# The end of a diffusion layer: last modulation as a row ahead of the turning, residual added in PSUM or by wide additions

## The chip, the cores and the metric

The kernel runs on one core of a Trainium2 chip. The metric is the device time of one execution in microseconds (us), lower is better. The engines of the core are named PE (matrix products; PEld is its weight load), DVE, ACT, POOL and SP (which mostly issues DMAs). PE writes to PSUM, a memory of eight banks of 128 partitions x 512 fp32 values; the other data lies in SBUF (128 partitions) or in HBM.

## The reference

One layer of a hybrid backbone, on 128 context tokens and 256 latent tokens, D_MODEL = 2048, all fp32. What matters here is the end:

```python
mod = jax.nn.silu(cond) @ lw['w_ada'] + lw['b_ada']
sh1, sc1, ga1, sh2, sc2, ga2 = [m[:, None, :] for m in jnp.split(mod, N_MOD, axis=-1)]
...
x = x + ga1 * rmsnorm(m, lw['norm_post_mix'])
h = rmsnorm(x, lw['norm_pre_ffn']) * (1.0 + sc2) + sh2
ff = (jax.nn.silu(h @ lw['w_ffn_gate']) * (h @ lw['w_ffn_up'])) @ lw['w_ffn_down']
x = x + ga2 * rmsnorm(ff, lw['norm_post_ffn'])
```

`cond` is one vector for all context tokens and another for all latent tokens, so the last factor, `ga2` times the gain of the norm, is one row of 2048 values for each of the two kinds. RMSNorm divides each token's row by the root of its mean square.

## The kernel before

**Tiling.** The 384 tokens are three blocks `t` of 128: block 0 is the context, blocks 1 and 2 are latent. The 2048 columns are 16 groups of 128 (index `k`) or 4 pieces of 512 (index `n` or `q`). Most of the kernel, and the residual `x1b` too, keeps columns on partitions and tokens along the free dimension; the output `yT` has that layout as well. The down projection of the FFN, in contrast, has tokens on partitions: `unit(t, n)` is the SBUF tile of 128 tokens x 512 columns in which the result of block `t`, piece `n`, is summed. So the end of the kernel has to *turn* each unit by PE, in four squares of 128x128.

**Weights.** They arrive by DMA as `raw` tiles of 512 KB in two buffers (L1654) or in resident slots `u...` (L1662). ACT rounds a tile to its high half `whi` (L1684), DVE subtracts to get the low half `wlo` (L1695), four buffers of each; PE multiplies high by high, high by low and low by high (L339). The FFN runs in 11 chunks of 512 hidden columns; steps "A" to "H" are the gate and up products, "D" the down product. In the order of pieces (0, 2, 1, 3) the last chunk's down product adds into the units; `add_last` (L1852, L1853) does this for a piece and has ACT sum the squares.

**The last modulation.** `ada_last` computes it in four quarters and leaves it in `mods[:, 5, k, c]`: partition = column within group `k`, `c` = 0 for context and 1 for latent. Its last write is DVE's at L1744. The resident slots 6 and 7 share the buffer `adacc` of an earlier phase.

**The end.** From `rest = d_order[2:]` on, the order on all engines and on SP is the order in which the code stands, as written by hand. Ahead of that line this holds for the other engines, while SP's DMAs are put in order by a scheduler, from when it expects their buffers and data to be ready. The last two pieces (1 and 3) are multiplied block by block (`last_products`), and the end of one block lies beside the products of the next:

- `norm(t)`: `most` and `factor` (root, ACT) and `inverse` (DVE) give the factor `r3[:, t]` of each token; `scale` multiplies the four pieces of the block by it, two on DVE (L1967), two on ACT (L1965).
- `turn(t, q)`: PE transposes the four squares of a piece (L1979) into one PSUM bank `py`. For block 2, pieces 0 and 2 are not scaled first: their squares are multiplied by `dg`, the identity times the factors, which turns and scales in one (L1981).
- `finals(t, q)`: for each of the four squares one DVE instruction, `x1b = py * mods + x1b` (`final`, L1992, 128x128). In some pieces ACT multiplies and POOL adds. For piece 3 of block 2 ACT multiplies four squares into `wide` (L2048) and DVE adds once (L2054).
- `store`: one DMA of 256 KB from SP for each piece (L1996), one from ACT.

PSUM banks come from two pools, `psm` with three and `pss` with five.

## Time and profile before

| what | value |
|---|---|
| median of 3 runs | 1921.23 us (1920.87 to 1922.34) |
| profiled execution, device time | 1922.69 us |
| its span in the trace | 1920.9 us |
| clock granted to PE | 1.0 |
| HBM read, written | 361.94 MB, 16.78 MB |
| mean DMA rate | 203 GB/s |

The profile is of one execution. "Span" is the time from its first to its last event in the trace; the device time has a little around it. Busy shares are means over the whole span, and the tail with which the change deals is under 1% of it, so it has to be read from the timeline and from windows of a few us. A row of the timeline gives start, duration, engine, line, operation, tiles, shape and, where instructions were merged, a count; in brackets stands how long the engine had been idle and what ended that. The chain of work is followed back from the last instruction, at each step to what released it.

### The profile page before, as it was taken

To read this page: it belongs to the slowest core of one execution; us is meant where nothing else is said; L and a number is where in the kernel's file an instruction comes from. 1 tells how busy PE (TensorE), PEld (TensorE's weight loads), DVE (VectorE), ACT (ScalarE), POOL (GpSimd) and SP (SyncE) were. 2 spreads that over 40 slices of the span, in tenths; PEclk is the share of its full clock that TensorE was granted. 3 is DMA by queue.
4 is the path that set the end of the run, shared out by engine and by line. 5 is a ranking of instruction groups with operands and counts; after the bars stand their busy time and mean duration, and the time that the engine had idled before them with its cause. 6 is when DMAs were issued, how large, how long until landed. Compare 5 with 4: busy or idle time off the path is not lost.

```text
span 1920.9 us, 27361 instructions
## 1 busy us (share of the span) xinstructions
PE 1901.7 (99%) x10318; PEld 1676.6 (87%) x10318; DVE 1650.9 (86%) x2168; ACT 999.4 (52%) x1428; POOL 82.7 (4%) x146
## 2 busy tenths in 40 slices
PE   8999999999999999999999999999999999999998
PEld 5679999999999999999988888888888788888886
DVE  5659897889868898987789989998998999887876
ACT  4235455545455654456456474556455545564544
POOL 0001111100000000104000000000000000000000
PEclk9999999999999999999999999999999999999999
DMA  9976766766657886656255656464746474736344
GB/s 390 400 280 226 261 224 227 269 211 207 215 180 236 285 297 227 211 201 224 68 178 160 189 148 199 142 191 143 224 127 210 122 229 114 221 92 198 92 153 145
DMA packets 237865, 389.70 MB, mean 203 GB/s; under 512 B 51189, under 2 KB 163925, under 8 KB 233381
## 3 DMA queue, kind: packets, MB, share of 16 engines
q1 hardware_dynamic: 218500, 330.02, 51.9%
q0 software_dynamic: 13952, 50.39, 8.5%
q10 hardware_dynamic: 5280, 7.55, 1.1%
q8 instruction: 81, 1.33, 0.3%
q14 instruction: 52, 0.42, 0.1%
HBM read 361.94 MB, written 16.78 MB: 197 GB/s over the span
## 4 chain that ended last, share of the span: by engine, by line
PE 84%; DVE 8%; DMA 4%; ACT 2%; issue 2%; SPq 0%; DVEq 0%; ACTq 0%
PE pmm L327 31%; PE pgu L339 24%; PE pdn L339 16%; PE pv L507 3%; DVE wlo L1695 2%; PE pgm L490 1%; DMA slab<-in_w_ada 1%; PE pf L1260 1%; PE pfo L1060 1%; PE pmm L1537 1%; DMA raw<-in_w_d 1%; DMA raw<-in_w_g 1%; ACT whi L1684 1%; DVE acc L1724 1%; DVE wlo L288 1%
## 5 line engine op out<-in xcount | busy, mean ns | idle before, releaser
L327 PE MATMUL pmm<-A_hi,whi 128*128 128x384 f32 x1088 | 366.9, 337 | 0.0
L327 PE MATMUL pmm<-A_hi,wlo 128*128 128x384 f32 x1088 | 364.2, 335 | 0.8 <-DVE wlo L288 0.8
L327 PE MATMUL pmm<-A_lo,whi 128*128 128x384 f32 x1088 | 364.1, 335 | 0.3 <-DVE A_lo L380 0.3
L1684 ACT CAST whi<-u 128x1024 fp32r<-128x1024 f32 x200 | 209.7, 1052 | 200.1 <-DVE u L1694 60.9
L1684 ACT CAST whi<-raw 128x1024 fp32r<-128x1024 f32 x175 | 183.8, 1050 | 189.8 <-DMA raw<-in_w_g 66.0
L1695 DVE TENSOR_TENSOR wlo<-u,whi 128x1024 fp32r<-128x1024 f32 x200 | 243.8, 1219 | 27.1 <-ACT whi L1684 21.3
L339 PE MATMUL pgu<-whi,A_lo 128*128 128x512 f32 x640 | 249.0, 389 | 0.0
L339 PE MATMUL pgu<-whi,A_hi 128*128 128x512 f32 x640 | 249.0, 389 | 0.0
L1695 DVE TENSOR_TENSOR wlo<-raw,whi 128x1024 fp32r<-128x1024 f32 x175 | 213.1, 1218 | 28.2 <-ACT whi L1684 18.7
L288 DVE TENSOR_TENSOR wlo<-raw,whi 128x1024 fp32r<-128x1024 f32 x165 | 200.6, 1219 | 31.0 <-ACT whi L301 30.7
L301 ACT CAST whi<-raw 128x1024 fp32r<-128x1024 f32 x151 | 157.9, 1049 | 123.2 <-PE pmm L327 42.9
L724 DVE SCALAR_TENSOR_TENSOR adacc<-adaw,spad,adacc 128x1024 f32<-128x1024 f32 x170 | 210.3, 1277 | 1.9 <-DMA adaw<-in_w_ada 1.7
L327 PEld LDWEIGHTS pmm<-A_hi,whi 128*128 128x128 f32 x1088 | 204.2, 188 | 3.3 <-issue 1.7
L327 PEld LDWEIGHTS pmm<-A_hi,wlo 128*128 128x128 f32 x1088 | 204.2, 188 | 1.4 <-DVE wlo L288 1.3
L327 PEld LDWEIGHTS pmm<-A_lo,whi 128*128 128x128 f32 x1088 | 204.4, 188 | 1.0 <-DVE A_lo L380 0.8
L339 PE MATMUL pdn<-whi,hid_hi 128*128 128x512 f32 x480 | 187.1, 390 | 0.6 <-DVE psums L1859 0.6
L339 PE MATMUL pgu<-wlo,A_hi 128*128 128x512 f32 x640 | 184.6, 390 | 2.2 <-DVE wlo L1695 2.2
L339 PE MATMUL pdn<-whi,hid_lo 128*128 128x512 f32 x480 | 186.8, 389 | 0.0
L339 PEld LDWEIGHTS pgu<-wlo,A_hi 128*128 128x128 f32 x640 | 119.7, 188 | 28.8 <-DVE wlo L1695 4.2
L339 PEld LDWEIGHTS pgu<-whi,A_hi 128*128 128x128 f32 x640 | 120.1, 188 | 25.0
L339 PEld LDWEIGHTS pgu<-whi,A_lo 128*128 128x128 f32 x640 | 120.1, 188 | 24.9
L339 PE MATMUL pgu<-whi,S 128*128 128x512 f32 x480 | 128.3, 389 | 0.0
(404 smaller groups left out, 3061.2 us busy)
## 6 DMA issues: line engine op xcount, KB each, us to landing
adaw<-in_w_ada POOLq DMA_DIRECT2D x96, 512.0 KB, 4.1
raw<-in_w_d SPq DMA_DIRECT2D x88, 512.0 KB, 3.9
slab<-in_w_ada SPq DMA_DIRECT2D x32, 1024.0 KB, 10.0
raw<-in_w_gate SPq DMA_DIRECT2D x64, 512.0 KB, 4.5
raw<-in_w_g SPq DMA_DIRECT2D x48, 512.0 KB, 3.7
raw<-in_w_u SPq DMA_DIRECT2D x48, 512.0 KB, 3.9
raw<-in_w_in SPq DMA_DIRECT2D x46, 512.0 KB, 4.3
u<-in_w_u SPq DMA_DIRECT2D x40, 512.0 KB, 4.7
```

The lines of the kernel that those rows point to most:

```text
L288: eng.tensor_sub(lo, raw, hi.bitcast(F32))
L301: ACT.copy(hi, raw)
L327: PE.matmul(dst, w[wi][:, k * n + n0 : k * n + n0 + P], x[xi][:, k0 + k, :], start=first and k == 0 and j == 0, stop=last and k == kts - 1 ...
L339: PE.matmul(dst, stat[x_][m], mov(w[w_], m), start=first and w_ == m == x_ == 0, stop=last and w_ == m == 1,)
L490: PE.matmul(pgv[q : q + 32, :], spad[:, k, :], slab[k // (KT // 2)][:, k % (KT // 2), :], start=k < 4, stop=k >= KT - 4,)
L507: PE.matmul(pv[2 * t + g], hT[x_][:, kb, t * P : (t + 1) * P], w_[:, g * 512 : (g + 1) * 512], start=kb == 0 and j == 0, stop=kb == KT - 1 ...
L724: DVE.scalar_tensor_tensor(acc[:, c, :], w, spad[:, k, c : c + 1], acc[:, c, :], op0=ALU.mult, op1=ALU.add,)
L1060: PE.matmul(p, w_of[0][:, i, k, g, :], x[:, :, lo:hi], start=kt == 0, stop=False)
L1260: PE.matmul(pf[:, 0 : 2 * HT], w[0][:, c], x[k], start=k == 0, stop=False)
L1537: PE.matmul(hp[u], hw[u][j][:, ((k - 1) % 8) * P : ((k - 1) % 8 + 1) * P], h2[m][:, k - 1, :], start=k == 1 and j == m == 0, stop=k == KT ...
L1684: ACT.copy(hi, src)
L1695: DVE.tensor_sub(lo, src, hi.bitcast(F32))
```

## The change

The latent row of the last modulation is written to HBM as a row (`m_d`, 2048 values, from `mods` with its columns on partitions) once `ada_last` is done, and is read back onto all 128 partitions as `mrow` (128x2048, in the buffer `adacc`) where `x1b` is loaded. In blocks 1 and 2, whose tokens all have this row, units can now be multiplied by it ahead of turning, as tokens x columns: `times_m`, or one fused instruction with the factor for block 1, piece 3. Pieces 0 and 1 of block 1 are turned and finished as before, with `mods`; so is all of block 0.

For four pieces (block 1: 2, 3; block 2: 1, 3) PE first puts the residual into the bank by a product of the identity with 512 columns of `x1b` (`old`), and the turning products add to it; ACT copies the bank to `x1b`. For pieces 0 and 2 of block 2 DVE adds the whole bank to `x1b` in one instruction. All of block 2 is turned by `dg`, so its units are not scaled.

```diff
+                mrow = adap.tile([P, D], F32, tag="adacc", name="mrow")
+                SP.dma_start(mrow, m_d.to_broadcast([P, D]))
                 ACT.activation(tmp1, eps_t, AF.Sqrt)
...
                 for _ in ada:
                     pass
+                m_d = dram.tile([1, D], F32, name="m_d")
+                SP.dma_start(m_d.rearrange("o (k p) -> (o p) k", p=P), mods[:, 5, :, 1])
...
-        def turn(t, q, diag=None):
-
+        def bank_of(t, q):
             pool = py_pools[t][q]
             py[t, q] = pool.tile([P, 4, P], F32, tag="side" if pool is pss else "mm", name="py")
+
+        def old(t, q):
+
+            bank_of(t, q)
+            PE.matmul(py[t, q], ident, y_of(t, q), start=True, stop=False)
+
+        def turn(t, q, diag=None):
+
+            added = (t, q) in py
+            if not added:
+                bank_of(t, q)
             for j in range(4):
                 src = unit(t, q)[:, j * P : (j + 1) * P]
                 if diag is None:
                     PE.transpose(py[t, q][:, j, :], src, ident)
                 else:
-                    PE.matmul(py[t, q][:, j, :], src, diag, start=True, stop=True)
+                    PE.matmul(py[t, q][:, j, :], src, diag, start=not added, stop=not added or j == 3)
+
+        def y_of(t, q):
+            return x1b[:, 4 * q : 4 * q + 4, t * P : (t + 1) * P]
+
+        def times_m(t, n):
+            DVE.tensor_mul(unit(t, n), unit(t, n), mrow[:, 512 * n : 512 * n + 512])
...
-            for n in range(4):
-                scale(ACT if n > 1 else DVE, t, n)
...
+        for t, n in ((2, 0), (1, 2), (2, 2)):
+            times_m(t, n)
         last_products(0, 0)
...
         norm(0)
+        for n in range(4):
+            scale(ACT if n > 1 else DVE, 0, n)
...
         norm(1)
+        scale(DVE, 1, 0)
+        scale(ACT, 1, 1)
+        scale(ACT, 1, 2)
+        f = unit(1, 3)
+        DVE.scalar_tensor_tensor(f, f, col(r3, 1), mrow[:, 3 * 512 :], op0=ALU.mult, op1=ALU.mult)
...
         add_last(2, rest[1], bk[2, 1], 3)
-        for q in range(2, 4):
-            turn(1, q)
+        times_m(2, 1)
+        for q in (2, 3):
+            old(1, q)
+            turn(1, q, ident)
+        for q in (1, 3):
+            old(2, q)
         factor(2)
-        finals(1, 2)
-        store(8, 12, 1, 2)
         inverse(2)
         DVE.tensor_scalar_mul(dg, ident, col(r3, 2))
-        scale(ACT, 2, 3)
-        scale(ACT, 2, 1)
-        finals(1, 3)
-        for q in (0, 3, 1, 2):
-            turn(2, q, dg if q in (0, 2) else None)
-        store(12, 16, 1, 2)
-        wide = ep[4].rearrange("p (j x) -> p j x", j=4)
-        for k in range(12, 16):
-            ACT.mul(wide[:, k - 12, :], py[2, 3][:, k - 12, :], mods[:, 5, k, 1:2])
-        finals(2, 0)
-        store(0, 4, 2, 3)
-        finals(2, 1)
-        store(4, 8, 2, 3)
-        last = x1b[:, 12:16, 2 * P : 3 * P]
-        DVE.tensor_add(last, last, wide)
-        store(12, 16, 2, 3, ACT)
-        finals(2, 2)
-        store(8, 12, 2, 3)
+        times_m(2, 3)
+        for q in range(4):
+            turn(2, q, dg)
+        for q in (2, 3):
+            ACT.copy(y_of(1, q), py[1, q])
+            store(4 * q, 4 * q + 4, 1, 2)
+        for q in range(4):
+            if q % 2:
+                ACT.copy(y_of(2, q), py[2, q])
+            else:
+                DVE.tensor_add(y_of(2, q), y_of(2, q), py[2, q])
+            store(4 * q, 4 * q + 4, 2, 3, ACT if q == 3 else SP)
```

How this moves instructions, at three places. First PE, behind the last two products with the weights (`pdn`, L339) at the end of the program; `py` are the banks, `ep_7646` is `dg`, `psums` are the units; lines 1979 and 1981 of before, 1983 (`old`) and 1995 (`turn`) of the change:

```order
-L1979 MATMUL py<-ident,psums 128x128 x8
-L1981 MATMUL py<-ep_7646,psums 128x128 x4
-L1979 MATMUL py<-ident,psums 128x128 x8
-L1981 MATMUL py<-ep_7646,psums 128x128 x4
-L2125 UNCONDITIONAL_BRANCH
+L1983 MATMUL py<-x1b,ident 128x512
+L1995 MATMUL py<-ident,psums 128x128 x4
+L1983 MATMUL py<-x1b,ident 128x512
+L1995 MATMUL py<-ident,psums 128x128 x4
+L1983 MATMUL py<-x1b,ident 128x512 x2
+L1995 MATMUL py<-ep_7646,psums 128x128 x16
```

Sixteen transposes and eight products by `dg` became four products of 512 columns, eight products by the identity and sixteen by `dg`, and all four wide ones stand ahead of the first product by `dg`.

Second SP's queue, from the last loads of up-weights on to the last loads of down-weights (`raw<-in_w_d`); first before, then the change:

```order
L1654 DMA raw<-in_w_u 128x4x256 x2
L1654 DMA raw<-in_w_d 128x2x512 x4
L1871 DMA x1b<-x_d 128x1536
L1654 DMA raw<-in_w_d 128x2x512
L1871 DMA x1b<-x_d 128x1536
L1654 DMA raw<-in_w_d 128x2x512
L1871 DMA x1b<-x_d 128x1536 x2
L1654 DMA raw<-in_w_d 128x2x512 x4
```

```order
L1654 DMA raw<-in_w_u 128x4x256 x2
L1654 DMA raw<-in_w_d 128x2x512
L1873 DMA mrow<-m_d 128x2048
L1654 DMA raw<-in_w_d 128x2x512 x2
L1871 DMA x1b<-x_d 128x1536
L1654 DMA raw<-in_w_d 128x2x512 x2
L1871 DMA x1b<-x_d 128x1536 x2
L1654 DMA raw<-in_w_d 128x2x512
L1871 DMA x1b<-x_d 128x1536
L1654 DMA raw<-in_w_d 128x2x512 x4
```

The load of `mrow` came between the first and the second of these down-weight loads, and the first and third pieces of `x1b` stand one weight load earlier.

Third SP's queue where the modulation has been completed, amid the products of the FFN:

```order
 L1654 DMA raw<-in_w_d 128x2x512
 L1662 DMA u_9282<-in_w_u 128x4x256
+L1925 DMA m_d<-mods 128x16x1
 L1654 DMA raw<-in_w_u 128x4x256
 L1662 DMA u_9280<-in_w_g 128x4x256
```

The store of `m_d` stands ahead of a load of up-weights, and nothing else moved there.

## The prediction

> **What bounds the kernel now.** I read the page's busy shares first, then the chain of work that ended last, then the timeline of the last 15 us.
>
> ```profile
> span 1920.9 us, 27361 instructions
> PE 1901.7 (99%) x10318; PEld 1676.6 (87%) x10318; DVE 1650.9 (86%) x2168; ACT 999.4 (52%) x1428; POOL 82.7 (4%) x146
> ```
>
> PE has work nearly everywhere, so before the end only what makes PE wait can move the time. The change works in the tail, after the last big products. There the chain of work leaves PE:
>
> ```profile
> 1874.65 26.63 PE pdn L339 x116
> ...
> 1909.70 0.60 DVE psums L1852
> ...
> 1910.38 0.73 ACT ep L1853 x2
> ...
> 1911.14 0.30 ACT r L1957
> ...
> 1911.66 0.30 DVE ep L2039
> ...
> 1912.09 1.15 PE py L1981 x8
> ...
> 1913.53 1.63 DVE x1b L1992 x6
> ...
> 1915.42 0.60 DVE x1b L2054
> 1916.02 1.04 DVE x1b L1992 x4
> ```
>
> Columns are start, duration, what. The last block's sum of squares is closed (1910.38), its root taken (1911.14), `dg`, the identity times the row factors, is ready at 1911.96, PE turns the blocks, and DVE finishes with the 128x128 `final` operations of L1992 until 1917.06. The last store is issued there (its row is below) and the span ends 3.84 us later. I take these 3.84 us as they are. So today the tail from 1912 is **DVE-bound**: DVE runs nearly without a gap, while PE is done at 1915.
>
> ```profile
> 1912.00:1915.00 3.00, 2.90 (x24) 2.73 (x24) 2.72 (x11) 2.14 (x6) 0.00 (x0) 1.00 0.81 235
> 1915.00:1918.00 3.00, 0.00 (x0) 0.00 (x0) 2.06 (x7) 0.00 (x0) 0.00 (x0) 1.00 0.83 237
> L1996 SPq DMA_DIRECT2D out_yT<-x1b x11: 372/373/492, 1905.3 to 1917.1; - x11
> ```
>
> (The windows give PE, PEld, DVE, ACT, POOL busy, then the clock: 1.00, no throttling. The third row gives the first and last start of a store.)
>
> **The change, part by part.** On DVE 20 `final` operations of the second and third token blocks go; two wide additions come in place of one, with five multiplications by `mrow` and one fused scale. ACT loses two scalings of 128x512 and four 128x128 multiplications, and gains four copies of 128x512. PE gets the residual of four 128x512 pieces (`old`), and 24 small matmuls by a diagonal, where it had 16 transposes and 8 such matmuls. So the question is what PE's list behind its last product costs.
>
> ```profile
> 1908.78 0.62 PE L339 MATMUL pdn<-wlo,hidE 128*128 128x512 f32 x2
> 1909.24 1.03 PE L1979 MATMUL py<-ident,psums 128*128 128x128 f32 x8
> 1913.93 1.06 PE L1981 MATMUL py<-ep,psums 128*128 128x128 f32 x8
> L1981 PE MATMUL py<-ep,psums x16: 275/275/348, 1912.1 to 1914.7; 128*128 128x128 f32 x16
> 8.72 4.68 PE L408 MATMUL px<-spad,ones 128*128 128x384 f32 x14
> L408 PE MATMUL px<-spad,ones x22: 486/486/980, 4.2 to 12.9; 128*128 128x384 f32 x22
> ```
>
> *Small matmuls.* The 8 matmuls of L1981 left 16 records: a full fp32 matmul is two records, a transpose only one (L1979). Eight records take 1.06 from the first start to the last end and one lasts 0.275, so they follow each other every (1.06 - 0.275) / 7 = 0.112 us. 24 matmuls are 48 records: 48 x 0.112 = **5.38 us**.
>
> *`old`.* No fp32 matmul of 512 columns stands in the trace. The widest has 384 columns (L408): (4.68 - 0.486) / 13 = 0.323 us per record. By columns, 512 give 0.43, so one `old` is 0.86 and four are **3.44 us**. The bound below is the 512-column product of L339, in a narrower fp32 form: its pair takes 0.62 with one lasting 0.39, thus 0.23 per record, 1.84 for four. The bound above is that records don't overlap: 0.486 x 512 / 384 = 0.65 each, 5.2. I take 3.44, since L408 has `old`'s type; the ends of the sum below are then +0.2 and +3.6 us.
>
> *The sum.* In PE's order nothing stands between the last product and `old`; the first can start where the transposes start today, 1909.24. Its bank was freed by the addition of L1852 at 1907.27 (row below). PE works 3.44 + 5.38 = 8.82 us to 1918.06, and the last record ends 0.16 later, 1918.22. Is another chain later? `dg` today is ready at 1911.96; PE arrives at the first matmul that needs it at 1909.24 + 3.44 + 16 x 0.112 = 1914.47. So 2.5 us of slack stand on the norm chain, and **PE becomes the bound of the tail**. Then comes ACT's copy of the last piece:
>
> ```profile
> 1871.56 1.56 ACT L1844 CAST hidE<-ptr 128x512 fp32r<-128x512 f32 x3
> 1915.34 0.68 DVE L2054 TENSOR_TENSOR x1b<-x1b,ep 128x512 f32<-128x512 f32 x1
> ```
>
> ACT reads three PSUM tiles of this size in 1.56, some 0.52 each, 0.6 standing alone (estimated between that and DVE's 0.68); with 0.05 to hand over, the copy ends at 1918.87. The other three pieces finish ahead: their PE results come 0.9 us apart, and one wide addition or copy is shorter. End of the last operation: 1917.06 becomes 1918.87, **+1.8 us**.
>
> *Ahead of the tail on DVE.*
>
> ```profile
> 1903.36 0.88 DVE L1967 TENSOR_SCALAR psums<-psums,r 128x512 f32<-128x512 f32 x2
> 1904.16 3.19 DVE L1992 SCALAR_TENSOR_TENSOR x1b<-py,mods,x1b 128x128 f32<-128x128 f32 x12
> 1907.27 0.68 DVE L1852 TENSOR_TENSOR psums<-psums,pdn 128x512 f32<-128x512 f32 x1
> ```
>
> The second scaling of L1967 becomes the fused one with `mrow`: 0.68 like DVE's other two-operand rows of this width instead of some 0.44, so DVE runs about 0.2 late and `dg` comes at 1912.2. The 2.5 us cover it. Three multiplications stand before the last weight split:
>
> ```profile
> 1889.51 1.88 DVE L1852 TENSOR_TENSOR psums<-psums,pdn 128x512 f32<-128x512 f32 x3 [1.89 <-PE pdn L339]
> 1891.81 0.63 ACT L1853 ACTIVATE ep<-psums 128x512 f32<-128x512 f32 x1
> 1893.50 1.22 DVE L1695 TENSOR_TENSOR wlo<-raw,whi 128x1024 fp32r<-128x1024 f32 x1 [2.11 <-ACT whi L1684]
> ```
>
> DVE idles 2.11 us there. The first two multiplications fit behind 1891.4; the third waits for the squares that read its block (1891.81 + 0.63) and ends at about 1893.1, before 1893.50. Cost 0; the next thing hurt would be PE's last weights, needed at 1895.2, 0.5 us after that split.
>
> *The new loads.* `mrow` (1 MB into SBUF) is issued once its buffer is freed by the split at 1853.99, ahead of the weight load at 1857.50:
>
> ```profile
> 1853.99 1.22 DVE L1695 TENSOR_TENSOR wlo<-u,whi 128x1024 fp32r<-128x1024 f32 x1
> 1857.50 0.37 SPq L1654 DMA_DIRECT2D raw<-in_w_d  x1
> 1854.00:1858.00 4.00, 4.00 (x19) 3.31 (x18) 3.94 (x5) 2.11 (x2) 0.00 (x0) 1.00 0.00 0
> 1861.32 1.05 ACT L1684 CAST whi<-raw 128x1024 fp32r<-128x1024 f32 x1 [2.14 <-DMA raw<-in_w_d]
> 1869.09 0.48 PE L339 MATMUL pdn<-whi,hid_hi 128*128 128x512 f32 x1
> slab<-in_w_ada SPq DMA_DIRECT2D x32, 1024.0 KB, 10.0
> ```
>
> The DMA engines are idle from 1854 to 1858 (share 0.00), and the weights loaded at 1857.50, split by 1863.6, are first used by PE at 1869.09 (counting the ten remaining blocks back from the last). That is 5.5 us of slack. Even at the 10 us of the slab load, which ran beside another stream, the block would be split by about 1868.7. Cost 0. The first and third pieces of the residual load now each overtake one weight load; those blocks have more slack still (the first is split at 1869.7 and used at 1877.98 on the same count). Nothing else on SP's queue moves.
>
> `m_d`, the store of the modulation as a row, writes 2048 separate 4-byte elements:
>
> ```profile
> 1664.71 0.17 DVE L1744 TENSOR_TENSOR mods<-mods,norms 128x8 f32<-128x8 f32 x1
> 1667.17 0.37 SPq L1654 DMA_DIRECT2D raw<-in_w_u  x1
> 1673.53 1.22 DVE L1695 TENSOR_TENSOR wlo<-raw,whi 128x1024 fp32r<-128x1024 f32 x1
> 1680.63 1.07 PE L339 MATMUL pgu<-wlo,A_hi 128*128 128x512 f32 x4
> q1 hardware_dynamic: 2786, 0.70, 18.9%
> ```
>
> It can go at 1664.9, and the next weight load is issued at 1667.17. That load is split by 1674.75 and its low half is used at 1680.63 by the same count, so `m_d` may hold the engines for 2.3 + 5.9 = 8.2 us before PE waits. The nearest row (DMA queues of the window 1687 to 1706) is of three DMA transposes in 19 us: 2786 packets of under 512 B took 18.9% of it, 3.6 us on each of 16 engines, for 174 packets each: 0.0206 us a packet. At that price 128 elements per engine take 2.6 us, hidden. But those packets did not write 4 bytes to HBM, so the price is unknown upward; below zero nothing can be won. I take 0.
>
> The Trainium skill, "DMA: Bandwidth & Descriptors", in Specifications says that transfers below 512 B are done by read-modify-write, and under Rules for kernel authors that a strided last dimension becomes one descriptor per element; its Latency section gives 0.2 us for an average HBM access. If the 128 elements of an engine went one after the other at that figure, an estimate from the page is 25.6 us, 17 us beyond the slack; by the transposes' row it is nothing. No run yet shows such a write.
>
> **Rivals.**
> 1. *`old` is cheap.* At 0.23 a record PE reaches the `dg` matmuls at 1909.24 + 1.84 + 1.79 = 1912.9 and ends at 1912.9 + 3.58 + 0.16 = 1916.6; with the copy 1917.3, +0.2 us: 1921.4. Against it: L408 shows 0.323 already at 384 columns.
> 2. *Slower: `m_d` blocks the weight queue.* It decides from 8.2 / 128 = 0.064 us per element. At 0.1 us the stall is 12.8 - 8.2 = 4.6 us, and with the tail 1921.23 + 4.6 + 1.8 = 1927.6. For it: the element is far smaller than any packet here. Against it: three times the transposes' price is needed. It is also the case that the Trainium skill's rule would bring, by a larger amount.
> 3. *The change shortens the tail as its words suggest*, PE's work being hidden. Even so the 16 `dg` matmuls after 1912.2 take 3.58 + 0.16, the copy 0.65: 1916.6, or -0.5 us: 1920.7. Faster by 0.2% (3.8 us) would need the last operation at 1913.2, before the second piece is turned.
>
> **How the numbers follow.** The sum stands against the profiled execution, 1922.69 us in all with a span of 1920.9; +1.8 gives 1924.5 there. That execution is 1.5 above the median 1921.23, so I forecast 1921.23 + 1.8 = **1923.0 us**. A measurement here can tell about 0.2%, 3.8 us, from no change: the forecast is "same". Chances: forecast 0.65 (1922.3 to 1924), rival 1 0.13, rival 2 0.12, rival 3 0.05, and 0.05 for the cover ahead of the tail failing by up to 3 us. The range reaches from rivals 1 and 3 to the beginnings of rival 2: 1920.6 to 1925.8. Faster by over 0.2%: 0.02 (out of rival 3); slower: 0.13 (rival 2, and a part of the last case); same: 0.85.
>
> **What would show it.** Right: PE busy without a gap from 1909.2 to about 1918.2, `old` in two records of 0.43 spacing, the chain's last steps PE and then ACT's copy, `dg` ready over 2 us before it is used. Wrong: a gap of PE before the `dg` matmuls (rival 1 or 3), or a PE wait near 1680 with a weight load landing late behind `m_d` (rival 2), or PE idle near 1869 behind `mrow`.

## The result, and the profile after

| | before | after |
|---|---|---|
| median, same chip | 1922.28 us (1920.26 to 1923.58, 12 runs) | 1926.70 us (1923.31 to 1928.75, 12 runs) |
| profiled execution, its span | 1922.69, 1920.9 us | 1924.47, 1922.7 us |
| ratio of the times | | 1.0024, 95% interval 1.0016 to 1.0032 |

The change made the kernel slower, by 4.4 us between the medians and 4.6 us by the ratio (3.1 to 6.2), just over the 0.2% that can be told apart. The forecast was 1923.0, the range ended at 1925.8. The profiled execution shows only 1.8 us of it: it was faster than ten of the twelve runs. A group of instructions that ends ahead of everything that the change touches shows where the rest went (its row of before, then of after; the two times are its first and last start):

```profile
L1724 DVE SCALAR_TENSOR_TENSOR acc<-w,spad,acc x120: 737/744/749, 986.2 to 1635.0; 128x512 f32<-128x512 f32 x120
```

```profile
L1724 DVE SCALAR_TENSOR_TENSOR acc<-w,spad,acc x120: 744/747/754, 985.8 to 1632.9; 128x512 f32<-128x512 f32 x120
```

This execution of after was already 2.1 us ahead. Such scatter is in every pair of traces, so the parts below are read as waits and stretches inside one trace, and the ratios stand beside them.

The end first. These are the last pieces of the chain of work of after (start, duration, what):

```profile
1909.63 0.86 PE py L1983 x2
1910.48 0.89 PE py L1995 x8
1911.38 0.86 PE py L1983 x2
1912.24 0.89 PE py L1995 x8
1913.13 1.72 PE py L1983 x4
1914.85 3.59 PE py L1995 x32
1918.43 0.02 issue
1918.45 0.58 ACT x1b L2077
```

And three rows of its timeline, the first `old`, `dg`, and the products by `dg`:

```profile
1909.46 1.02 PE L1983 MATMUL py<-x1b,ident 128*128 128x512 f32 x2
1912.15 0.29 DVE L2068 TENSOR_SCALAR ep<-ident,r 128x128 f32<-128x128 f32 x1
1914.68 3.73 PE L1995 MATMUL py<-ep,psums 128*128 128x128 f32 x32
```

PE works without a gap from 1909.46, one `old` takes 0.86 us in two records, `dg` is ready at 1912.44 and waits 2.2 us for PE, and ACT's copy ends at 1919.03. Before, the same stretch ran from 1909.24 to 1917.06. Counted from the start of the end's PE work, the last operation comes at 9.57 us instead of 7.82: **+1.75 us**.

Then a place where before has no wait at all. These are rows of after's timeline: SP's issue of the new store, the two loads behind it, and the first instructions that those loads let go (in brackets the idle time before, and what ended it):

```profile
1662.82 0.37 SPq L1925 DMA_DIRECT2D m_d<-mods  x1
1665.06 0.84 SPq L1654 DMA_DIRECT2D raw<-in_w_u  x1
1666.32 0.37 SPq L1662 DMA_DIRECT2D u<-in_w_g  x1
1677.32 1.04 ACT L1684 CAST whi<-raw 128x1024 fp32r<-128x1024 f32 x1 [9.43 <-DMA raw<-in_w_u]
1678.42 0.50 PE L339 MATMUL pgu<-whi,A_hi 128*128 128x512 f32 x1 [1.64 <-ACT whi L1684]
```

PE's waits from 1640 to 1900 (us in total, times, longest), and from before's page the usual time of such a load (KB each, us from issue to landing):

```profile
PE pgu L339 <- ACT whi L1684: 1.6, 1, 1.6
PE pdn L339 <- DVE hidE L1844: 0.5, 1, 0.5
```

```profile
raw<-in_w_u SPq DMA_DIRECT2D x48, 512.0 KB, 3.9
```

The up-weights issued at 1665.06 reach ACT at 1677.3, 12 us later, and PE stands still for 1.64 us. Of the wait on `hidE`, near 1874, 0.3 us was there before and 0.2 us are new. So the trace holds 1.75 + 1.6 + 0.2 = 3.6 us of the 4.4 to 4.6.

### The profile page after: what moved, and what is told of

Read it like the earlier page. It is cut to its first block, busy times and chain, and to the rows that moved or that the text cites. A ratio compares the mean times of both kernels' runs of the same rounds, so it can differ in the third digit from the quotient of the medians.

```text
span 1922.7 us, 27395 instructions
## 1 busy us (share of the span) xinstructions
PE 1906.5 (99%) x10342; PEld 1680.3 (87%) x10342; DVE 1650.0 (86%) x2154; ACT 997.8 (52%) x1426; POOL 82.9 (4%) x146
## 3 DMA queue, kind: packets, MB, share of 16 engines
q10 hardware_dynamic: 5280, 7.55, 1.1%
## 4 chain that ended last, share of the span: by engine, by line
PE 87%; DVE 6%; DMA 3%; ACT 2%; issue 1%; SPq 0%; DVEq 0%; ACTq 0%
PE pmm L327 31%; PE pgu L339 26%; PE pdn L339 17%; PE pv L507 3%; PE pgm L490 1%; DVE wlo L1695 1%; DMA slab<-in_w_ada 1%; PE pf L1260 1%; PE pfo L1060 1%; PE pmm L1537 1%; DMA raw<-in_w_u 1%; DVE wlo L288 1%; DVE adacc L724 1%; ACT whi L1684 1%; PE pf L1261 1%
## 5 line engine op out<-in xcount | busy, mean ns | idle before, releaser
L1695 DVE TENSOR_TENSOR wlo<-u,whi 128x1024 fp32r<-128x1024 f32 x200 | 244.2, 1221 | 25.6 <-ACT whi L1684 21.5
L339 PE MATMUL pgu<-whi,A_hi 128*128 128x512 f32 x640 | 249.1, 389 | 1.6 <-ACT whi L1684 1.6
L339 PE MATMUL pgu<-whi,A_lo 128*128 128x512 f32 x640 | 249.0, 389 | 0.0
L339 PE MATMUL pdn<-whi,hid_hi 128*128 128x512 f32 x480 | 187.0, 390 | 0.0
L339 PE MATMUL pdn<-whi,hid_lo 128*128 128x512 f32 x480 | 186.8, 389 | 0.0
L339 PE MATMUL pgu<-wlo,A_hi 128*128 128x512 f32 x640 | 184.6, 390 | 1.9 <-DVE wlo L1695 1.9
L339 PEld LDWEIGHTS pgu<-wlo,A_hi 128*128 128x128 f32 x640 | 119.6, 188 | 28.4 <-DVE wlo L1695 3.9
L339 PEld LDWEIGHTS pgu<-whi,A_hi 128*128 128x128 f32 x640 | 120.1, 188 | 26.9 <-ACT whi L1684 2.1
L339 PEld LDWEIGHTS pgu<-whi,A_lo 128*128 128x128 f32 x640 | 120.1, 188 | 24.9
L339 PE MATMUL pgu<-whi,S 128*128 128x512 f32 x480 | 128.3, 389 | 0.0
```

The lines of the kernel that those rows point to most:

```text
L339: PE.matmul(dst, stat[x_][m], mov(w[w_], m), start=first and w_ == m == x_ == 0, stop=last and w_ == m == 1,)
L1695: DVE.tensor_sub(lo, src, hi.bitcast(F32))
```

## The experiments

Each ratio is to the kernel before, run beside it, with its 95% interval. Theory A in the first four expectations is that the end costs its 1.9 us by itself and the store of 4-byte pieces the rest.

### One part at a time

tail_only: after without the store; `mrow` is filled from the input xT.

```diff
-SP.dma_start(mrow, m_d.to_broadcast([P, D]))
+SP.dma_start(mrow, a["xT"][0:1].rearrange("p k t -> p (k t)")[:, 0:D].to_broadcast([P, D]))
...
-m_d = dram.tile([1, D], F32, name="m_d")
-SP.dma_start(m_d.rearrange("o (k p) -> (o p) k", p=P), mods[:, 5, :, 1])
```

> The change without the store of m_d; mrow is loaded, at the same place, from a row of the input xT, so that the last modulation of the latent blocks is left out of the result. Theory A (the time is the longer PE list of the tail, some 1.9 us, plus a PE wait of 2 to 3 us behind the 4-byte store near 1665-1680 us): no PE wait over 0.5 us in that stretch, and +1.9 us against the kernel before (ratio 1.0010). Rival B (the tail alone, or the load of mrow, costs all of it in the timed runs): +4.4 us (1.0023), as the change itself.

Measured: 1.0010 (1.0001 to 1.0018). The start of the end's PE work and its last operation:

```profile
1909.48 1.02 PE L1981 MATMUL py<-x1b,ident 128*128 128x512 f32 x2
1918.47 0.58 ACT L2075 COPY x1b<-py 128x512 f32<-128x512 f32 x1 [1.20 <-PE py L1993]
```

And the window at the store's place (its length, then PE's busy time):

```profile
1660.00:1700.00 40.00, 40.00 (x178) 33.10 (x178) 35.02 (x39) 25.16 (x34) 0.00 (x0) 1.00 0.49 148
```

9.57 us as in after, and PE busy for all of 1660 to 1700. The end costs its 1.8 us with no store, and the 0.5 us on `hidE` is there too.

store_only: before, plus the store alone.

```diff
+m_d = dram.tile([1, D], F32, name="m_d")
+SP.dma_start(m_d.rearrange("o (k p) -> (o p) k", p=P), mods[:, 5, :, 1])
```

> The kernel before with the store of m_d alone added, at the same place; nothing reads it. Theory A: the next load of up-weights lands some 12 us after its issue instead of 4, PE waits 1 to 3 us for its high or low half near 1675-1680 us, and +2.5 us (ratio 1.0013). Rival B: the store is hidden in the mean, 0 +- 1 us (1.0000).

Measured: 1.0011 (1.0002 to 1.0020). PE's waits are shorter than expected: 0.4 and 0.3 us on `whi` near 1678 and 1682, and 0.4 on `wlo` near 1711. The end alone at 1.0010 and the store alone at 1.0011 add up to the whole, 1.0024, within the intervals.

store_twice: after, with the same store issued a second time, into a second row.

```diff
 SP.dma_start(m_d.rearrange("o (k p) -> (o p) k", p=P), mods[:, 5, :, 1])
+m_e = dram.tile([1, D], F32, name="m_e")
+SP.dma_start(m_e.rearrange("o (k p) -> (o p) k", p=P), mods[:, 5, :, 1])
```

> The change with the 4-byte store issued twice in a row, the second into another row of HBM that nothing reads. Theory A: the first store uses up the slack of the weight loads (8.2 us by the trace of before), so the second one adds its whole 8 to 9 us to PE's wait: +12 to +13 us against before (ratio 1.0065). Rival B: at most +1 us more than the change, +5 us (1.0027).

Measured: 1.0067 (1.0054 to 1.0081). PE's wait:

```profile
PE pgu L339 <- ACT whi L1684: 8.9, 1, 8.9
```

And the two windows behind it (the third number from the end is the granted clock):

```profile
1685.00:1690.00 5.00, 2.37 (x6) 1.89 (x7) 3.23 (x3) 2.84 (x3) 0.00 (x0) 0.50 0.82 285
1690.00:1695.00 5.00, 5.00 (x19) 4.00 (x18) 4.93 (x7) 3.33 (x5) 0.00 (x0) 0.79 0.91 261
```

The ratio came as expected. The wait grows by 7.3 us, from 1.6 to 8.9, a little less than the 8 to 9 expected, and behind it PE is granted 0.50 and 0.79 of its clock.

### Is it the number of pieces?

store_quarters: the store in four parts of 512 pieces, each as soon as its four groups of factors are there.

```diff
+part = m_d[:, 512 * q : 512 * q + 512].rearrange("o (k p) -> (o p) k", p=P)
+SP.dma_start(part, mh[:, :, 1])
...
-SP.dma_start(m_d.rearrange("o (k p) -> (o p) k", p=P), mods[:, 5, :, 1])
```

> The change with m_d stored in four parts, each when its quarter of the modulation is done (512 elements of 4 bytes, 32 per DMA engine, some 2 us of the queue each). Theory A: each part stays within the slack of the weight loads, no PE wait over 0.5 us behind any of them, and only the tail's +1.9 us is left (ratio 1.0010). Rival B: as the change, +4.4 us (1.0023).

Measured: 1.0034 (1.0021 to 1.0046), if anything slower than after: theory A missed, and the rival's 1.0023 lies at the lower end. The parts went out at 1129, 1307, 1490 and 1668. The fourth has no wait behind it; the third fell ahead of a place near 1510 at which PE waits in before too. This is that wait in before, store_quarters, and two kernels below, rows_after and store_half, which write no part of `m_d` within 200 us ahead of it; the last row is the window behind it in store_quarters:

```profile
1510.94 0.50 PE L339 MATMUL pgu<-wlo,A_hi 128*128 128x512 f32 x1 [1.00 <-DVE wlo L1695]
```

```profile
1513.62 0.79 PE L339 MATMUL pgu<-wlo,A_hi 128*128 128x512 f32 x1 [2.37 <-DVE wlo L1695]
```

```profile
1509.29 0.98 PE L339 MATMUL pgu<-wlo,A_hi 128*128 128x512 f32 x3 [1.86 <-DVE wlo L1695]
```

```profile
1509.32 0.98 PE L339 MATMUL pgu<-wlo,A_hi 128*128 128x512 f32 x2 [2.04 <-DVE wlo L1695]
```

```profile
1510.00:1515.00 5.00, 2.63 (x9) 1.88 (x8) 5.00 (x7) 1.23 (x2) 0.00 (x0) 0.85 0.16 52
```

So this wait scatters from one execution to the next, by about as much as it grew, and how much of the 2.4 us belongs to the third part is not shown. It also moves single traces by a us or two, ahead of all that the change touches.

rows_after: one PE transpose and one ACT copy make 16 rows of 128 factors, stored as 16 pieces of 512 bytes.

```diff
+PE.transpose(pt[0:KT, 0:P], mods[:, 5, :, 1], ident)
...
+ACT.copy(mrows, pt[0:KT, 0:P])
+SP.dma_start(m_d.rearrange("o (k p) -> (o k) p", p=P), mrows)
...
-SP.dma_start(m_d.rearrange("o (k p) -> (o p) k", p=P), mods[:, 5, :, 1])
```

> The changed kernel, with the row of factors stored in another form: the 128x16 factors are turned by one TensorE transpose into 16 rows of 128 numbers, copied to SBUF by ScalarE, and stored as 16 pieces of 512 bytes instead of 2048 of 4 bytes. Nothing else differs; the output is the same. Theory (the 4-byte pieces hold the DMA engines about 9 us and make the weights behind them late): the wait of 1.64 us on whi at line 339 behind 1675 is gone, only the longer end of 1.9 us is left, ratio to before 1.0010, last operation of the end as in the changed kernel. Rival (a round trip through HBM at this place costs by itself, whatever its pieces, since the transfers and the queue stop for it): the ratio stays at 1.0020 to 1.0024, with a wait over 1 us on a weight tile within 15 us of the store.

Measured: 1.0027 (1.0017 to 1.0038). The wait near 1675 is gone, but so is the store from that place: the transpose stood late in PE's order, so the row was there only at 1868 and SP stopped 1.7 us for it; the 1 MB load of `mrow` moved from 1855 to 1870, next to the last weights, and a new wait came (the wait, then the window behind it):

```profile
PE pdn L339 <- ACT whi L1684: 1.8, 1, 1.8
```

```profile
1895.00:1900.00 5.00, 4.71 (x13) 3.48 (x14) 3.26 (x8) 2.11 (x7) 0.00 (x0) 0.66 0.00 0
```

The rival's number came, by another mechanism than the rival's. Two kernels take it apart. rows_early has these lines where the store stood in the code of after, so that the store goes out at 1832.8 and the load at 1853.8. mrow_late is tail_only with only the load held back to 1870, by a copy that stands late in the code:

```diff
+ACT.copy(mrow[:, 0:1], mods[:, 5, 0, 1:2])
...
 SP.dma_start(mrow, a["xT"][0:1].rearrange("p k t -> p (k t)")[:, 0:D].to_broadcast([P, D]))
```

> As rows_after (the row of factors stored as 16 pieces of 512 bytes), with the TensorE transpose and the copy some 190 us earlier, so that the store is issued at about 1846 and the 1 MB load of mrow stands in SP's order where it stands in the changed kernel (about 1855) and not behind the residual's loads (1870). Theory (the 4-byte pieces were one cost, and what rows_after paid in their place was the load of mrow at 1870, which held up the last weights): no wait of PE over 0.6 us behind 1660, neither near 1675 nor near 1893, and a ratio of 1.0010 by the end alone. Rival (the round trip through HBM costs wherever it stands): 1.0020 or more, with a wait of PE over 1 us behind the store or the load.

Measured: 1.0019 (1.0010 to 1.0028), between the two expectations, and the interval holds both 1.0010 and after's 1.0024. There is no wait for weights behind the store, but one of 0.8 us in which PE's transpose waits for a PSUM bank that DVE is reading. By the waits of these traces the remedy cost half of the 1.6 us that it saved.

> As tail_only (no m_d; mrow is loaded from the input xT, so the rows of blocks 1 and 2 are not the reference's), but the 1 MB load of mrow first waits for a ScalarE copy into its tile, so that it is issued behind the residual's loads at about 1870, as in rows_after. Theory (rows_after's loss is this load's place: 1 MB at 290 to 390 GB/s ahead of the last weights makes them about 3 us late): a wait of PE near 1893 of 1.5 to 2 us, a lower granted clock right behind it, and a ratio near 1.0025, against 1.0010 of tail_only. Rival (rows_after's loss came from its transpose, its copy or the queue's stop for m_d): no such wait, 1.0010.

Measured: 1.0012 (1.0003 to 1.0021): this theory fell, the load's place alone leaves one wait of 0.4 us. What rows_after lost took the stop of SP, or that and the load's place together; this was not separated further. A part of its 1.0027 may also be scatter: in its trace PE waits 1.86 us near 1510, where before waits 1.00. (The wait of 0.5 us on `hidE` near 1874 is not there in mrow_late, so it goes with the earlier place of these loads.)

store_half and two_halves: half of the factors stored (the other half of `mrow` comes from xT), and all of them as two stores of 1024 pieces.

```diff
-SP.dma_start(m_d.rearrange("o (k p) -> (o p) k", p=P), mods[:, 5, :, 1])
+SP.dma_start(m_d[:, 0 : D // 2].rearrange("o (k p) -> (o p) k", p=P), mods[:, 5, 0 : KT // 2, 1])
...
+if (kind, c, i) == ("D", NFC - 2, 5):   # from here on two_halves alone
+    SP.dma_start(m_d[:, D // 2 :].rearrange("o (k p) -> (o p) k", p=P), mods[:, 5, KT // 2 :, 1])
```

> The changed kernel with half of the factors stored (groups 0 to 7 of 16, 1024 pieces of 4 bytes); the other half of the row on all partitions comes from the input xT, so the output of columns 1024 and up is not the reference's. The end has the same instructions. Theory (a threshold: the weights have about 8 us of slack and the pieces take 0.07 us each on 16 engines, so half of them take 4.5 us and are hidden): no wait of PE over 0.8 us between 1660 and 1690, ratio 1.0010 by the end alone. Rival (each piece costs, with no slack that hides it): half of what the whole store cost, a wait of about 0.8 to 1 us there and a ratio of 1.0016.

> The changed kernel with its 4-byte store in two halves of 1024 pieces: groups 0 to 7 as soon as they are there, near 1307, groups 8 to 15 where the whole store was, near 1663. The output is the reference's. Theory (a threshold: a half holds the DMA engines about 4.5 us, less than the weights' slack at both places): no wait of PE over 0.8 us behind either, a ratio of 1.0010 to 1.0012. Rival (pieces cost wherever they are, and the third quarter of store_quarters was only the place where it showed): 1.0020 or more, with a wait over 1 us behind 1307 or 1663.

Measured: 1.0018 (1.0009 to 1.0027) and 1.0019 (1.0010 to 1.0028). The second store of two_halves went out at 1664.0, and PE's wait behind it is:

```profile
PE pgu L339 <- ACT whi L1684: 0.8, 1, 0.8
```

The half of store_half went out at 1306, as soon as its factors were there, so this run says nothing of the place at 1663; it shows no wait there, and why its ratio is above tail_only's is open (the intervals overlap; its trace has the 2.04 us near 1510). In two_halves 1024 pieces at 1664 made PE wait 0.8 us. With 2048 pieces the same instruction waited 1.6 us in after, 1.2 in after profiled once more (below) and 0.4 in store_only, so these waits don't show that fewer pieces cost less. The 4.5 us that the theory gave a half would have been hidden altogether.

### What happens behind the pieces

The DMA engines' packets in after (count, bytes, sizes), from 1664 to 1668, while the pieces are written:

```profile
DMA packets 2332, 0.27 MB, mean 68 GB/s; under 512 B 2073, under 2 KB 2332, under 8 KB 2332
```

From 1668 to 1674, behind them (the second row: the queue's packets, MB and share of 16 engines):

```profile
DMA packets 235, 0.23 MB, mean 39 GB/s; under 512 B 7, under 2 KB 235, under 8 KB 235
q1 hardware_dynamic: 235, 0.23, 79.7%
```

And in before, over the loads of the same place, from 1666 to 1680:

```profile
DMA packets 3154, 3.41 MB, mean 243 GB/s; under 512 B 107, under 2 KB 2895, under 8 KB 3152
q1 hardware_dynamic: 3152, 3.38, 75.1%
```

The 4-byte pieces are done by 1668. Behind them 235 weight packets keep the engines busy for 79.7% of 6 us: 0.797 x 6 x 16 / 235 = 0.33 us each. In before it is 0.751 x 14 x 16 / 3152 = 0.053. The engines are not held by the pieces; the weights that they read **afterwards come six times slower**, for some 6 us.

Fewer pieces leave the same stretch. These are the packets of store_quarters from 1673 to 1677, behind its fourth part of 512 pieces, and of two_halves from 1670 to 1674, behind 1024:

```profile
DMA packets 189, 0.19 MB, mean 48 GB/s; under 512 B 0, under 2 KB 189, under 8 KB 189
```

```profile
DMA packets 124, 0.13 MB, mean 32 GB/s; under 512 B 0, under 2 KB 124, under 8 KB 124
```

Read in windows of 0.5 us, the DMA engines are back above 200 GB/s 10 and 12 us after the issue of 512 pieces (the fourth part and the third), 11.5 us after that of 1024 or of 2048, and 19.5 us after the issue of the first of the two stores of store_twice. So from 512 pieces on the length goes with the number of stores, hardly with the number of pieces. That would also explain why four stores were no remedy, but this is only argued.

late_4byte and late_64byte put the store, from a tile of its own, ahead of another weight load; late_64byte stores the factors as they lie, 16 in a row per partition, in 128 pieces of 64 bytes.

```diff
-SP.dma_start(m_d.rearrange("o (k p) -> (o p) k", p=P), mods[:, 5, :, 1])
...
+DVE.tensor_copy(mcol, mods[:, 5, :, 1])
+SP.dma_start(m_d.rearrange("o (k p) -> (o p) k", p=P), mcol)   # late_4byte
+SP.dma_start(m_d.rearrange("o (p k) -> (o p) k", p=P), mcol)   # late_64byte
```

> The changed kernel with its store of 2048 pieces of 4 bytes, out of a tile of its own, moved to about 1846, some 3 us ahead of a weight load of 512 KB. The output is the reference's. Theory (what follows such a store within some 8 us is slowed, wherever it stands): that weight load lands in 7 to 12 us instead of about 4, and DMA moves 10 to 90 GB/s at a busy share over 0.4 for several us. Rival (the slow stretch belongs to the place near 1664, where four loads stand in the queue): the load lands in 4 to 5 us.

> As late_4byte, with the factors stored as they lie in SBUF, 16 in a row for each partition: 128 pieces of 64 bytes instead of 2048 of 4. The row is then in another order, so the output is not the reference's. If pieces of 4 bytes spread over the same short stretch of memory from many engines are the cause, the load behind lands in its usual 4 to 5 us; if any write of less than 512 bytes is, it lands as late as in late_4byte, 7 to 12 us.

They went out at 1834.7 and 1836.3, earlier than expected, 1.1 us ahead of a load. First late_4byte, its packets of 1835 to 1837 and of 1837 to 1845:

```profile
DMA packets 2064, 0.01 MB, mean 4 GB/s; under 512 B 2064, under 2 KB 2064, under 8 KB 2064
DMA packets 74, 0.15 MB, mean 19 GB/s; under 512 B 0, under 2 KB 0, under 8 KB 74
```

Its issues (KB each, us to landing) and PE's wait:

```profile
raw<-in_w_d SPq DMA_DIRECT2D x1, 512.0 KB, 12.6
m_d<-mcol SPq DMA_DIRECT2D x1, 8.0 KB, 11.7
```

```profile
PE pdn L339 <- ACT whi L1684: 2.0, 1, 2.0
```

Then late_64byte, its packets of 1837 to 1845, and its issues:

```profile
DMA packets 944, 1.06 MB, mean 132 GB/s; under 512 B 176, under 2 KB 688, under 8 KB 944
```

```profile
raw<-in_w_d SPq DMA_DIRECT2D x2, 512.0 KB, 3.5
m_d<-mcol SPq DMA_DIRECT2D x1, 8.0 KB, 1.4
```

Of the 4-byte store all packets pass in 2 us, yet it lands only after 11.7 us, and until then the load behind it crawls at 19 GB/s and lands after 12.6 us; PE waits 2.0 us. With 64-byte pieces the store lands in 1.4 us and the load in 3.5. The slow stretch follows the 4-byte store to another place, and it is gone with 128 larger pieces. This is one execution of each kernel; rows_early, whose 16 pieces of 512 bytes went out 2 us earlier, landed them in 1.4 us as well. But that fewer pieces and not larger ones did it is not excluded, since no run has so few pieces of 4 bytes. The stretch ends when the store lands: the rate is back above 200 GB/s at 1846.2, and 1834.7 + 11.7 is 1846.4. Which of the two brings about the other, and why, no run shows.

store_in_gap: the whole 4-byte store where before loads no weights, from 1771 to 1798. The instruction that copies the factors reads a finished hidden tile times 0, so that it can't run earlier.

```diff
+if c == NFC - 2:
+    pend.append(lambda: DVE.scalar_tensor_tensor(mcol, s5[:, 0:KT], 0.0, mods[:, 5, :, 1], op0=ALU.mult, op1=ALU.add))
+    pend.append(lambda: SP.dma_start(m_d.rearrange("o (k p) -> (o p) k", p=P), mcol))
...
-SP.dma_start(m_d.rearrange("o (k p) -> (o p) k", p=P), mods[:, 5, :, 1])
```

> The changed kernel with its whole store of 2048 pieces of 4 bytes moved to about 1785, where before has no weight load from 1771 to 1798, only DMA transposes: a small VectorE instruction copies the factors to a tile of their own once the last hidden third of that chunk is done, and the store reads that tile. The output is the reference's. Theory (the pieces are written in about 3 us and slow down what loads in the 7 us behind them, so that only a neighbour is hurt): no wait of PE over 0.8 us between 1640 and 1840, the weights at 1798 land in their usual 4 to 5 us, and the ratio is that of the end alone, 1.0010 to 1.0012, against 1.0024. Rival (the transposes behind the store are slowed as the weights were, and the hidden values that they turn come late): a wait of PE over 1 us on a hidden tile near 1800 and a ratio of 1.0020 or more.

Measured: 1.0010 (1.0001 to 1.0019), 1923.87 us. It was issued at 1780.0. These are the packets from 1781 to 1782 and from 1782 to 1783, and those of a DMA transpose from 1787 to 1789 with their share of 16 engines:

```profile
DMA packets 1496, 0.05 MB, mean 47 GB/s; under 512 B 1496, under 2 KB 1496, under 8 KB 1496
DMA packets 763, 0.00 MB, mean 3 GB/s; under 512 B 763, under 2 KB 763, under 8 KB 763
```

```profile
q1 hardware_dynamic: 1056, 0.26, 68.5%
```

Nothing follows the pieces until the transpose at 1787. It moves 7 to 9 us behind the issue, where weights crawl in the other traces, and takes 0.685 x 2 x 16 / 1056 = 0.021 us a packet, as the transposes of before in the prediction: it is not slowed. Whether a load would have been at that moment this trace can't show. PE has no wait from 1640 to 1840 (its one wait up to 1900 is the 0.5 us of tail_only), and the ratio is tail_only's. The same 2048 pieces are free here.

after_again is after itself, profiled once more.

> The changed kernel itself, profiled a second time, since its first profiled execution (1924.47 us) was faster than 10 of its 12 runs and shows only 1.8 us of the 4.6 us between the medians. Theory (two costs, the end's 1.9 us and a wait behind the 4-byte store that depends on how far the weights were ahead when it began): the last operation ends 9.6 us behind the start of the end's TensorE work as before, and the wait on whi behind 1675 is there again, of 1.6 to 4 us; ratio 1.0020 to 1.0026. Rival (the wait was an accident of one execution): no wait over 0.8 us between 1660 and 1690 though the ratio stays above 1.0016, so that the rest of the time went to a place not yet named.

Measured: 1.0023 (1.0013 to 1.0032), and the wait is there again, shorter than expected:

```profile
PE pgu L339 <- ACT whi L1684: 1.2, 1, 1.2
```

Its last operation:

```profile
1922.36 0.59 ACT L2077 COPY x1b<-py 128x512 f32<-128x512 f32 x1 [1.20 <-PE py L1995]
```

The last operation comes 9.6 us behind the start of the end's PE work, as in after. This execution was the slowest of its ten runs, 1928.41 us with a span of 1926.6, 5.7 us longer than before's. Of these, 1.2 + 0.2 + 1.8 = 3.2 us are the wait, the loads and the end, and 1.6 us were lost ahead of 1640 (the group of L1724 has its last start at 1636.6); 0.9 us were not located.

### Can the end be lighter?

light_end (as rows_after, with `old` only for (2,1) and (2,3); DVE adds the residual of (1,2) and (1,3)) and lightest_end (`old` only for (2,1); (2,2) and (2,3) scaled by ACT and DVE and turned by plain transposes).

```diff
         for q in (2, 3):
-            old(1, q)
-            turn(1, q, ident)
+            turn(1, q)
...
         for q in (2, 3):
-            ACT.copy(y_of(1, q), py[1, q])
+            DVE.tensor_add(y_of(1, q), y_of(1, q), py[1, q])
```

lightest_end has these lines too, and further:

```diff
-        for q in (1, 3):
-            old(2, q)
+        old(2, 1)
...
-        times_m(2, 3)
-        for q in range(4):
-            turn(2, q, dg)
+        f = unit(2, 3)
+        DVE.scalar_tensor_tensor(f, f, col(r3, 2), mrow[:, 3 * 512 :], op0=ALU.mult, op1=ALU.mult)
+        scale(ACT, 2, 2)
+        turn(2, 1, dg)
+        turn(2, 0, dg)
+        turn(2, 3)
+        turn(2, 2)
...
```

> As rows_after, and with less TensorE work in the end: of the four blocks to which TensorE adds the residual only (2,1) and (2,3) are left; blocks (1,2) and (1,3) are turned by plain transposes and their residual is added by wide VectorE additions. Theory (the end is bound by TensorE from its last product on, and each residual block costs it 0.86 us): two blocks less are 1.7 us less, PE has (1,2), (1,3), two residual blocks and then 16 turns by dg behind the last product, 1.78 + 1.72 + 3.59 = 7.1 us, and the last ScalarE copy ends at about 7.7 us behind it against 9.4 in the changed kernel: ratio to before 1.0001, 1.7 us below rows_after. Rival (the end is bound by VectorE and ScalarE, or by the stores behind them, once TensorE is lighter): the VectorE additions push the last ones back and it gains 0.8 us or less on rows_after, ratio 1.0006 or more.

> As light_end, with one residual block (2,1) left on TensorE, in its wait for the factor; pieces (2,2) and (2,3) are scaled by ScalarE and by a fused VectorE instruction while TensorE turns (2,1) and (2,0), and are turned by plain transposes; VectorE adds all residuals but one. Theory: TensorE ends 1.78 + 0.86 + a wait of 0.2 + 3.59 = 6.4 us behind its last product and VectorE adds the last block in 0.7 us, the last operation at 7.1 us against 9.4 in the changed kernel and 7.5 in the one before: ratio to before 0.9998. Rival (VectorE, with nine wide operations from the factor on, ends last): its 0.7 us each end near 8 us, and it is no faster than light_end, 1.0001 or more.

Measured: 1.0018 (1.0009 to 1.0027) and 1.0025 (1.0015 to 1.0035). Both carry rows_after's wait near 1893, so 1.0027 is their measure. ACT's last copy in light_end:

```profile
1919.24 0.58 ACT L2080 COPY x1b<-py 128x512 f32<-128x512 f32 x1 [1.20 <-PE py L1999]
```

The window in which its stores run out (the last two numbers are the DMA engines' busy share and GB/s):

```profile
1921.00:1923.00 2.00, 0.00 (x0) 0.00 (x0) 0.00 (x0) 0.00 (x0) 0.00 (x0) 1.00 0.95 277
```

And the same window in after:

```profile
1921.00:1923.00 2.00, 0.00 (x0) 0.00 (x0) 0.00 (x0) 0.00 (x0) 0.00 (x0) 0.50 0.04 12
```

The end's PE work starts at 1912.27 in light_end, so its last operation comes at 7.55 us against 9.57. The theory's 7.7 came out, and lightest_end's 7.07 against 7.1, but in part by luck. The theory counted the plain transposes of (1,2) and (1,3) as 1.78 us, the price of full products; they took 0.87. A wait of PE for `dg` made up for it, 0.4 us in light_end, where none was expected, and 1.2 in lightest_end instead of 0.2. And less of the gain reaches the end of the kernel. The stores of 256 KB, 0.9 us each at 280 GB/s, now come in one bunch and end 0.95 x 2 us into the window from 1921, 10.6 us behind that start; in after it is 11.6, in before 9.9 (1919.14 by the same reading). Of 2.0 us won by the engines 1.0 reaches the end. lightest_end is no better there, 10.7 us by the same reading. The ratios differ from rows_after's by less than their intervals, so the runs can't tell 1.0 us from the theory's 1.7. No version beat before.

## Why the prediction was wrong, step by step

- *What bounds the end* held. PE became the bound, `dg` waited 2.2 us (predicted 2.5), the last operation came 9.57 us behind the start of the end's PE work (predicted 1918.87 - 1909.24 = 9.63), and tail_only and store_in_gap put the end by itself at 1.0010. `old` came out at the predicted 0.43 us a record.
- *DVE ahead of the tail, cost 0*, held. *`mrow` and the moved residual loads, cost 0*, missed 0.2 us: PE's wait ahead of the last 116 products went from 0.3 to 0.5, and tail_only shows the same 0.5, mrow_late none.
- *`m_d`, cost 0*: **this step failed**. It priced the store by how long its pieces keep the engines, 0.0206 us each by the transposes' row, and took the 8.2 us of slack as enough. The pieces themselves were no dearer than that (2064 packets in 2 us). What the step left out is what goes on behind them: the store lands only after 11.7 us (late_4byte), and until then the weights behind it come at a sixth of their speed (39 instead of 243 GB/s in after). The slack was not enough for that. In place of 0 the store cost 2.1 us by the ratio of store_only and 2.7 by those of after and tail_only; as waits of PE 1.6 and 1.2 us of it stand in two traces of after and 1.1 in store_only.
- *Rival 2* named the place and the sign, and the wait on weights near 1680 was its mark. Its switch, 0.064 us per element, was the wrong quantity: quarters and halves show the slow stretch as well, and in the gap 2048 pieces cost nothing. That its 1927.6 us lies near the measured 1926.70 is luck: it had a stall of 4.6 us. The Trainium skill, "DMA: Bandwidth & Descriptors", Specifications, gives transfers below 512 bytes as read-modify-write; the direction agrees, but the 64-byte pieces are below that too, and behind them the load landed in 3.5 us as usual. The 25.6 us estimated from its Latency section were not seen: the packets passed in 2 us and the store landed after 11.7.
- *The base*: the median of before was 1921.23 in the three runs shown, and 1922.28 in the twelve beside after. Of the 3.7 us between forecast and result 1.05 are this and 0.2 the loads. That leaves 2.4 for the store, as the ratios have it; about 1 us of this is in none of the waits, which is less than the interval (1.5 us either way), and was not located. That some executions wait longer than those profiled, and then pay in clock too, would fit, but is only argued.

## What to carry to other kernels

Price a store not only by the time its packets take, but by the time until it lands and by what is queued behind it: put a store of tiny pieces where nothing loads for some 12 us, or make its pieces fewer and larger; splitting it into several stores did not help here. When work moves from a bound engine to another, add up the new engine's list from its last unavoidable product on, and then the stores that end behind it; here first PE, then the bunched stores took the gain. A remedy that needs an instruction on a busy engine (the transpose of rows_early) must be priced like the change itself.

## What the runs showed of the hardware that was not expected

- A store of 2048 pieces of 4 bytes to HBM: all packets done in 2 to 4 us, landing after 11.7 us (late_4byte), and weight packets behind it at 0.33 us each instead of 0.053 (after). 512 pieces leave a stretch of nearly the same length. A DMA transpose 7 to 9 us behind the issue was not slowed (0.021 us a packet, store_in_gap). With 128 pieces of 64 bytes: landing after 1.4 us.
- The granted clock can halve behind a short wait of PE. After 1.64 us in after and 1.71 near 1510 in store_twice it stays at 1.00. After 1.86 us (rows_after, near 1510), 2.04 (late_4byte, store_half) and 2.37 (store_quarters) it falls to 0.50. Between them both came: 0.66 over 5 us after 1.76 us in rows_after near 1895, but 1.00 behind 1.77 us in lightest_end (its row below) and behind the 1.82 us of before's own end. 0.66 over 5 us at 0.50 is 5 x 0.34 / 0.50 = 3.4 us of half clock, so such a wait costs PE another 1.7 us of work.

```profile
1895.00:1900.00 5.00, 4.04 (x16) 3.04 (x17) 3.70 (x9) 2.60 (x7) 0.00 (x0) 1.00 0.00 0
```
